# An encoder layer's MLP epilogue: squares and gate inputs of one chunk in instructions of 512 columns, one to a step

## The chip, the cores and the metric

The kernel runs on one core of a Trainium2 chip. The metric is device time in microseconds (us) of one launch; the time before is the median of three runs. A profile is one execution recorded instruction by instruction, with its own time. The engines are TensorE (PE, with its weight loads shown as PEld), VectorE (DVE), ScalarE (ACT), GpSimd (POOL) and SyncE (SP), which here issues the DMAs. Each engine works through its own instructions in program order.

## The reference

One layer of an encoder, applied to two sequences (512 and 1024 tokens, 1536 in all) with shared weights; the model width is 1024.

```python
h = h + concat(attention, pooling) @ w_out
m = _rmsnorm(h, norm_mlp_g)
h = h + jnp.square(jax.nn.relu(m @ w_up)) @ w_down
gate = jax.nn.sigmoid(_rmsnorm(h, norm_ple_g) @ w_ple_gate)
h = h + gate * (p_i @ w_ple_proj)
y = _rmsnorm(h, final_norm_g)
```

What matters here is the seam between the third and the fourth line. When the MLP of some tokens is done, the new `h` has to be squared and summed over the width (for the RMSNorm in front of the gate), and multiplied by the gain `norm_ple_g` (the gate's input).

## The kernel before

**Tiling.** The 1536 tokens form three chunks `c` = 0, 1, 2 of 512 tokens. `h` lies transposed: `hT[c][a]`, with `a` from 0 to 3, is a tile of 128 x 1024 numbers, two blocks `e` = 0, 1 of 128 channels by 512 tokens. A float32 product is made of three matmuls on float32r parts, a high and a low part of each operand (`three`); so every operand has to be split, high part on ACT by a rounding copy, low part on DVE or POOL by a subtraction. All working tiles come from one pool of 49 slots.

**The MLP loop.** The loop over `pairs` (48 of them, 16 to a chunk, numbered here from 0) does the MLP: a pair is two blocks of 128 columns of `w_up`. `Pair.run` forms the up-projection with seven half-size block products in the order 1, 6, 2, 5, 7, 3, 4 (PSUM tiles `px`, `py`, `px`, `pz`, `pq`, `pz`, `pq`), combines them on DVE into `c1` and `c2`, applies relu and square on ACT, and subtracts on DVE to get the low part of the result `r` (L886). Four times in a pair `between` is called, which runs `before.down(i)`: a quarter of the down-projection of the previous pair, into `pd`, added to `h` on DVE (L837). The first of these quarters, after product 1, is the first reader of the `r` that the pair before has just made: ahead of it lie c1's and c2's relu and squares (L875 to L877, L881 to L883) and L886.

**Steps.** After each of the seven products `after(i)` is called. It takes one piece of the stream that splits the next pair's up weights (`feeding`, ACT cast L786, POOL subtraction L787), one of the splits of the down weights, and one `step()`. `step()` advances the first generator in the queue `chores` by one `yield`. So a pair has seven steps; this text calls them places 0 to 6, place 0 being `after(1)`, place 4 `after(7)`, place 5 `after(3)` and place 6 `after(4)`. When a generator is used up, the same step already begins the next one in the queue.

**What is in the queue.** At the second pair of a chunk `c` (pairs 1, 17, 33) the queue gets, in this order: `invert(c)`, four steps; `finishing(c - 1)` if there was a chunk before; and `make_m(c + 1)` if there is a chunk after. `finishing` closes the MLP of the chunk before: for each of the four tiles it scales `h` back by `ws` (L1138, two instructions of 512 columns, one to a step), writes it out to DRAM (`hl_d`), squares it on ACT (L1142), and from the second tile on adds the square to a running sum on POOL (L1147, two steps). For chunk 0 it also makes the gate's input, high part on ACT (L1126) and low part on DVE (L1128, two steps), and writes both to `hg_d`. At the end come the last sum (L1155), waits of some steps, and `spread_g`, which turns the sum into a row of reciprocal roots. `make_m(c + 1)` prepares the MLP input of the next chunk in two halves of 22 steps: loads, squares (L607, L609), gains, differences, and the splits into `mm` (ACT L637, POOL L634), written to `mo_d`; then, seven steps on, a product for the sum, L646 on DVE, and the write of `w_d` (L647).

**The end of a chunk.** In the last pair of a chunk `after(i)` also loads the operands of the next chunk's products (`load_mo`, from `mo_d`). At the start of the next chunk `h` is loaded, `load_ms` loads `w_d` into `ws`, and `raise_h` multiplies `h` by it on DVE (L662). All these DMAs are issued by SP in program order.

Of the kernel before, what the change touches and what calls it, by code (L numbers as in the profile page):

```python
# [11 lines left out]
AF = mybir.ActivationFunctionType  # L12
# [23 lines left out]
def encoder_layer(ctx, tc, xT, xn, xr, pT, w1, w2, w_pool, w_out, w_up, w_down, w_gate, w_proj,  # L36
# [7 lines left out]
    ve, sc, gp, sy = nc.vector, nc.scalar, nc.gpsimd, nc.sync  # L44
# [15 lines left out]
    def as32(ap):  # L60
        return ap.bitcast(F32)

    def flat(ap):
        return as32(ap).rearrange("p a b -> p (a b)" if len(ap.shape) == 3 else "p a b c -> p (a b c)")
# [9 lines left out]
    def slot(shape, dt, name):  # L74
        n = math.prod(shape[1:])
        full = slots.tile([P, SLOT], dt, tag="s", name=name)
        v = full[:, 0:n]
        if len(shape) == 3:
            v = v.rearrange("p (a b) -> p a b", a=shape[1])
        elif len(shape) == 4:  # L80
            v = v.rearrange("p (a b c) -> p a b c", a=shape[1], b=shape[2])
        return v
# [432 lines left out]
    def wait(n):  # L515
        for _ in range(n):
            yield
# [165 lines left out]
    def spread_g(c, acc):  # L683
        bc = yield from rsqrt_rows([acc[:, 0]], CH, f"g{c}")
        if c != 1:
            bcs["t"] = slot([P, 2, CH], F32, f"bcs{c}")
        sc.copy(bcs["t"][:, c % 2], bc)
        bcs[c] = bcs["t"][:, c % 2]
        yield
# [428 lines left out]
    def gate_in(c, a, high=None, hs=range(2)):  # L1118

        if (c, a) not in gin:  # L1120
            gin[c, a] = [slot([P, 2, CH], F32R, f"hg{c}{a}_{i}") for i in range(2)]
        hl = gin[c, a]
        for h in hs:
            g = gple_sb[:, 2 * a + h:2 * a + h + 1]
            if high is not False:
                sc.activation(hl[0][:, h], hT[c][a][:, h], AF.Copy, scale=g)  # L1126
            if not high:
                ve.scalar_tensor_tensor(hl[1][:, h], hT[c][a][:, h], g, as32(hl[0][:, h]), op0=ALU.mult, op1=ALU.subtract)  # L1128

    hl_d = [[dram.tile([P, 2, CH], F32, name=f"hl_d{c}_{a}") for a in range(4)] for c in range(2)]  # L1130
    def finishing(c):


        acc = slot([P, 2, CH], F32, f"sqg{c}")
        for a in range(4):
            h = hT[c][a]
            for e in range(2):
                ve.tensor_tensor(h[:, e], h[:, e], ws[c], op=ALU.mult)  # L1138
                yield
            sy.dma_start(hl_d[c][a], h)  # L1140
            sq = slot([P, 2, CH], F32, f"sqg{c}{a}") if a else acc
            sc.activation(sq, h, AF.Square)  # L1142
            if c == 0:
                gate_in(0, a, True)
            yield
            for e in range(2) if a else ():
                gp.tensor_tensor(acc[:, e], acc[:, e], sq[:, e], op=ALU.add)  # L1147
                yield
            if c == 0:
                for e in range(2):  # L1150
                    gate_in(0, a, False, (e,))
                    yield
                for i in range(2):
                    sy.dma_start(hg_d[a][i], flat(gin[c, a][i]))
        gp.tensor_tensor(acc[:, 0], acc[:, 0], acc[:, 1], op=ALU.add)  # L1155
        yield from wait(6)
        yield from spread_g(c, acc)
# [22 lines left out]
    for n, pair in enumerate(pairs):  # L1180
        c, g = pair.c, pair.g
# [7 lines left out]
        if g == 1:  # L1189
            chores.append(invert(c))  # L1190
            if c:
                load_ms(c - 1)
                chores.append(finishing(c - 1))
            if c < 2:
                chores.append(make_m(c + 1, ve, gp))
# [105 lines left out]
    for c, o, w in groups:  # L1301
        sq = []
# [94 lines left out]
```

## Time and profile before

| What | Value |
|---|---|
| Time, median of 3 runs | 1814.47 us (1813.41 to 1815.92) |
| The profiled execution's own time | 1813.31 us |
| Its span | 1811.5 us |
| PE busy | 1759.7 us, 97% of the span |
| DVE, POOL, ACT busy | 1260.0, 1053.7 and 939.7 us |
| The eight squares of L1142, mean of one | 1058 ns |
| The 24 high parts of L1126, mean of one | 711 ns |

Times within the span are counted from its start. The MLP loop runs from about 579 us to 1620 us; chunk 1 begins at about 923 us and chunk 2 at about 1270 us. A row of a timeline gives start, duration, engine, line, operation, output and inputs, the number of instructions merged, and in brackets the idle time of the engine just before with what ended it. A row of windows gives for a stretch the busy time of each engine. Busy times can include waits of a pipelined matmul, so the distance between the same product of two pairs says more about PE's pace than its busy share.

### The profile page before, as it was taken

To read this page: it belongs to the slowest core of one execution; us is meant where nothing else is said; L and a number is where in the kernel's file an instruction comes from. 1 tells how busy PE (TensorE), PEld (TensorE's weight loads), DVE (VectorE), ACT (ScalarE), POOL (GpSimd) and SP (SyncE) were. 2 spreads that over 40 slices of the span, in tenths; PEclk is the share of its full clock that TensorE was granted. 3 is DMA by queue.
4 is the path that set the end of the run, shared out by engine and by line. 5 is a ranking of instruction groups with operands and counts; after the bars stand their busy time and mean duration, and the time that the engine had idled before them with its cause. 6 is when DMAs were issued, how large, how long until landed. Compare 5 with 4: busy or idle time off the path is not lost.

```text
span 1811.5 us, 28604 instructions
## 1 busy us (share of the span) xinstructions
PE 1759.7 (97%) x10540; PEld 1537.1 (85%) x10540; DVE 1260.0 (70%) x1843; ACT 939.7 (52%) x1854; POOL 1053.7 (58%) x923
## 2 busy tenths in 40 slices
PE   9999899999999799999999999999999999999997
PEld 7888777888868798988888889889898999888887
DVE  5677865888894677865568877876776556665655
ACT  6434455768794455655445545554455444443332
POOL 3474774535674567676656776785577666543121
PEclk9999999999999899999999999999999999999998
DMA  6333545120519335343364442556443323272102
GB/s 248 114 123 105 216 165 185 36 94 13 206 46 367 139 122 198 121 177 100 136 265 157 163 151 96 195 185 235 179 157 100 110 94 99 89 262 70 59 12 82
DMA packets 83883, 256.84 MB, mean 142 GB/s; under 512 B 9888, under 2 KB 16416, under 8 KB 83744
## 3 DMA queue, kind: packets, MB, share of 16 engines
q1 hardware_dynamic: 83744, 255.02, 39.7%
q8 instruction: 83, 1.36, 0.3%
q14 instruction: 56, 0.46, 0.1%
HBM read 195.74 MB, written 59.24 MB: 141 GB/s over the span
## 4 chain that ended last, share of the span: by engine, by line
PE 78%; DVE 7%; ACT 5%; DMA 3%; issue 3%; POOL 1%; POOLq 0%; DVEq 0%; ACTq 0%; SPq 0%
PE pd L49 25%; PE z L49 7%; PE px L49 6%; PE pz L49 6%; PE pq L49 6%; PE pg L49 6%; PE py L49 4%; PE pp L49 3%; PE o L49 3%; PE tp L53 3%; PE po L49 3%; PE S L49 3%; PE pj L49 1%; DMA wur<-in_w_up_dram 1%; DVE r L886 1%
## 5 line engine op out<-in xcount | busy, mean ns | idle before, releaser
L49 PE MATMUL pd<-r,wd 128*128 128x512 f32 x2304 | 568.5, 395 | 10.8 <-DVE r L886 10.6
L49 PEld LDWEIGHTS pd<-r,wd 128*128 128x128 f32 x2304 | 419.5, 188 | 100.3 <-DVE r L886 16.1
L787 POOL TENSOR_TENSOR w<-ws,w 128x512 fp32r<-128x512 f32 x192 | 272.5, 1423 | 217.9 <-ACT w L786 206.8
L787 POOL TENSOR_TENSOR w<-wur,w 128x512 fp32r<-128x512 f32 x144 | 212.8, 1489 | 135.4 <-ACT w L786 134.4
L837 DVE TENSOR_TENSOR h<-pd,h 128x1024 f32<-128x1024 f32 x192 | 233.5, 1216 | 76.6 <-PE pd L49 76.5
L786 ACT CAST w<-ws 128x512 fp32r<-128x512 f32 x192 | 118.5, 617 | 271.1 <-DVE ws L795 241.1
L461 POOL TENSOR_SCALAR pr<-pr,rr 128x512 f32<-128x512 f32 x160 | 111.2, 705 | 134.7 <-DVE rr L456 66.8
L49 PE MATMUL z<-w,x 128*128 128x512 f32 (+1 forms) x864 | 175.7, 359 | 0.9 <-DVE w L160 0.5
L49 PEld LDWEIGHTS pz<-mo,w 128*128 128x128 f32 x1152 | 150.7, 190 | 19.3 <-issue 11.2
L49 PEld LDWEIGHTS z<-w,x 128*128 128x128 f32 x864 | 142.9, 189 | 28.0 <-ACT w L159 2.1
L49 PE MATMUL pz<-mo,w 128*128 128x256 f32 x1152 | 153.6, 283 | 10.2 <-issue 10.2
L817 DVE TENSOR_TENSOR wd<-wdr,wd 128x512 fp32r<-128x512 f32 x96 | 102.8, 1071 | 83.1 <-ACT wd L816 76.6
L49 PE MATMUL pq<-mo,w 128*128 128x256 f32 x1152 | 153.7, 283 | 1.0 <-issue 1.0
L49 PE MATMUL px<-mo,w 128*128 128x256 f32 x1152 | 152.2, 281 | 0.0
L49 PEld LDWEIGHTS px<-mo,w 128*128 128x128 f32 x1152 | 146.5, 189 | 4.0
L49 PEld LDWEIGHTS pq<-mo,w 128*128 128x128 f32 x1152 | 144.7, 191 | 1.4 <-issue 1.3
L49 PE MATMUL pg<-hg,wg 128*128 128x512 f32 (+1 forms) x768 | 141.0, 338 | 0.2
L472 ACT CAST pt<-tp 128x512 fp32r<-128x512 f32 x160 | 88.0, 591 | 88.5 <-PE tp L53 86.8
L49 PEld LDWEIGHTS pg<-hg,wg 128*128 128x128 f32 x768 | 118.6, 188 | 17.8 <-DVE hg L1128 1.0
L817 POOL TENSOR_TENSOR wd<-wdr,wd 128x512 fp32r<-128x512 f32 x96 | 131.8, 1373 | 2.6 <-DMA w_d<-sqm 2.6
L886 DVE TENSOR_TENSOR r<-c,r 128x512 fp32r<-128x512 f32 x96 | 74.7, 783 | 74.1 <-ACT c L883 46.2
L473 DVE TENSOR_TENSOR pt<-tp,pt 128x512 fp32r<-128x512 f32 x160 | 104.0, 684 | 31.4 <-ACT pt L472 31.1
(195 smaller groups left out, 3036.2 us busy)
## 6 DMA issues: line engine op xcount, KB each, us to landing
wur<-in_w_up_dram SPq DMA_DIRECT2D x96, 512.0 KB, 4.2
wdr<-in_w_down_dram SPq DMA_DIRECT2D x96, 512.0 KB, 4.4
mo_d<-mm SPq DMA_DIRECT2D x84, 256.0 KB, 2.3
mo<-mo_d SPq DMA_DIRECT2D x42, 512.0 KB, 7.7
h_d<-h SPq DMA_DIRECT2D x16, 512.0 KB, 3.0
h<-h_d SPq DMA_DIRECT2D x16, 512.0 KB, 9.9
xn<-in_xn_dram SPq DMA_DIRECT2D x12, 512.0 KB, 6.4
qs_d<-qs SPq DMA_DIRECT2D x12, 512.0 KB, 3.0
```

What stands on the lines that cost most here:

```text
L49: last_pe[0] = nc.tensor.matmul(*a, **k).ins
L53: last_pe[0] = nc.tensor.transpose(*a, **k).ins
L461: gp.tensor_scalar(p, p, rr, 1.0, op0=ALU.mult, op1=ALU.mult)
L472: sc.copy(self.pt[kt][:, 0], tp)
L473: ve.tensor_tensor(self.pt[kt][:, 1], tp, as32(self.pt[kt][:, 0]), op=ALU.subtract)
L786: sc.copy(t[:, 0], x)
L787: gp.tensor_tensor(t[:, 1], x, as32(t[:, 0]), op=ALU.subtract)
L817: (gp, ve)[i].tensor_tensor(lo, self.dr[i][:, h], as32(hi), op=ALU.subtract)
L837: ve.tensor_tensor(h, pd.rearrange("p (a b) -> p a b", a=2), h, op=ALU.add)
L886: ve.tensor_tensor(self.r[i][:, 1], x, as32(self.r[i][:, 0]), op=ALU.subtract)
```

## The change

In `finishing` the square of a tile, one instruction of 1024 columns, becomes two of 512 columns, each with a step of its own. For chunk 0 the two instructions that make the high part of the gate's input, issued before in the same step as the square, get a step each as well.

```diff
             sy.dma_start(hl_d[c][a], h)
             sq = slot([P, 2, CH], F32, f"sqg{c}{a}") if a else acc
-            sc.activation(sq, h, AF.Square)
-            if c == 0:
-                gate_in(0, a, True)
-            yield
+            for e in range(2):
+                sc.activation(sq[:, e], h[:, e], AF.Square)
+                yield
+            for e in range(2) if c == 0 else ():
+                gate_in(0, a, True, (e,))
+                yield
             for e in range(2) if a else ():
                 gp.tensor_tensor(acc[:, e], acc[:, e], sq[:, e], op=ALU.add)
                 yield
```

`gate_in(0, a, True, (e,))` issues L1126 for the block `e` alone. Nothing else is changed, and the numbers computed are the same. `finishing(0)` has 38 steps in its four tiles where it had 26, `finishing(1)` 22 where it had 18; chunk 2 doesn't use `finishing`.

## The prediction

> **What bounds the kernel now.** I read the page first, then the stretch in which `finishing` runs, by waits, by the timeline and by the distance of equal products. The page:
>
> ```profile
> span 1811.5 us, 28604 instructions
> PE 1759.7 (97%) x10540; PEld 1537.1 (85%) x10540; DVE 1260.0 (70%) x1843; ACT 939.7 (52%) x1854; POOL 1053.7 (58%) x923
> ```
>
> PE sets the time: only what makes it wait can be won back, and a change on ACT alone is worth nothing where PE runs on. The waits between 950 and 1070 us, where `finishing(0)` runs, show what is to be won there (total, times, longest):
>
> ```profile
> PEld pd L49 <- DVE r L886: 4.8, 3, 1.8
> ```
>
> Three times the down-projection waits for the low part of `r`. One of the three, in pair 20, from the timeline of all engines:
>
> ```profile
> 1028.22 0.62 ACT L786 CAST w<-ws 128x512 fp32r<-128x512 f32 x1 [4.49 <-DVE ws L795]
> 1028.75 1.06 ACT L1142 ACTIVATE sqg<-h 128x1024 f32<-128x1024 f32 x1
> 1029.25 0.41 DVE L874 TENSOR_TENSOR c<-pz,u 128x256 f32<-128x256 f32 x1
> 1029.71 1.32 ACT L1126 ACTIVATE hg<-h,gple_sb 128x512 fp32r<-128x512 f32 x2
> 1030.93 0.40 ACT L875 ACTIVATE c<-c 128x256 f32<-128x256 f32 x1
> ...
> 1033.71 1.27 PE L49 MATMUL pd<-r,wd 128*128 128x512 f32 x4
> 1034.46 0.63 ACT L883 ACTIVATE c<-c 128x512 f32<-128x512 f32 x1
> 1034.63 1.27 POOL L1147 TENSOR_TENSOR sqg<-sqg,sqg 128x512 f32<-128x512 f32 x1
> 1035.12 1.32 DVE L886 TENSOR_TENSOR r<-c,r 128x512 fp32r<-128x512 f32 x1 [1.61 <-ACT c L883]
> 1036.50 2.15 PE L49 MATMUL pd<-r,wd 128*128 128x512 f32 x8 [1.52 <-DVE r L886]
> ```
>
> The relu L875 has its input at 1029.66 (1029.25 + 0.41), but ACT has the step's square and two gate inputs in front of it and starts L875 at 1030.93: 1.27 us late. From there ACT has no pause up to L883, DVE subtracts last, and PE stands for 1.52 us. In pairs 18, 19 and 20 this step falls on place 4, just ahead of that chain; in pair 17 on place 6, behind it, and PE doesn't wait.
>
> What a pair loses is read from the distance of its first `px` to that of the next pair. The rows below are those of pairs 2 and 5, 19 to 22, 26 and 27, 36 and 37:
>
> ```profile
> 624.85 1.60 PE L49 MATMUL px<-mo,w 128*128 128x256 f32 x12
> ...
> 688.15 1.58 PE L49 MATMUL px<-mo,w 128*128 128x256 f32 x12
> ...
> 987.06 1.59 PE L49 MATMUL px<-mo,w 128*128 128x256 f32 x12
> 1009.22 1.57 PE L49 MATMUL px<-mo,w 128*128 128x256 f32 x12
> 1032.29 1.59 PE L49 MATMUL px<-mo,w 128*128 128x256 f32 x12
> 1055.34 1.57 PE L49 MATMUL px<-mo,w 128*128 128x256 f32 x12
> ...
> 1141.05 1.56 PE L49 MATMUL px<-mo,w 128*128 128x256 f32 x12
> 1163.96 1.59 PE L49 MATMUL px<-mo,w 128*128 128x256 f32 x12
> ...
> 1356.92 1.57 PE L49 MATMUL px<-mo,w 128*128 128x256 f32 x12
> 1379.17 1.57 PE L49 MATMUL px<-mo,w 128*128 128x256 f32 x12
> ```
>
> Pairs 2, 3 and 4 take (688.15 - 624.85) / 3 = 21.10 us each: an undisturbed pair. The three pairs from 987.06 to 1055.34 take 68.28, which is 4.98 more than 3 x 21.10. The pair at 1356.92, in `finishing(1)`, takes 22.25, so 1.15 too many. The pair at 1141.05, in `make_m(2)`, takes 22.91 and loses 1.81.
>
> **The change part by part.** First the work itself, from the groups with each shape apart:
>
> ```profile
> L1126 ACT ACTIVATE hg<-h,gple_sb 128x512 fp32r<-128x512 f32 x24 | 15.3, 711 | 0.0
> L607 ACT ACTIVATE sqm<-m 128x512 f32<-128x512 f32 x24 | 15.2, 634 | 0.0
> L1142 ACT ACTIVATE sqg<-h 128x1024 f32<-128x1024 f32 x8 | 8.5, 1058 | 0.0
> ```
>
> Removed are 8 squares of 1058 ns; added are 16 of 634 ns (L607 is the same operation at 512 columns): 10.1 for 8.5 us, 1.7 us more ACT work over some 20 pairs, where ACT is little over half busy. Its price is nothing as long as no piece stands in the chain ahead of L886.
>
> [...]
>
> *finishing(0): 4.98 us, of which 4.4 go.* The 2.4 us lump becomes four steps of 0.63 or 0.71. Counting yields from place 0 of pair 17 (four of `invert`, then 8 for the first tile and 10 for each other, two of them L1138 ahead of the square), the four ACT steps fall on these places: first tile 6, 0, 1, 2; second 0, 1, 2, 3; third 3, 4, 5, 6; fourth 6, 0, 1, 2. Places 6 and 0 to 3 are covered: the chain is over by then, and ahead of place 4 ACT idles 4.49 us (the first row of the timeline). The third tile, in pair 20, keeps 0.63 on place 4, which fits the 0.8 us between the end of L786 (1028.84) and L875's input (1029.66), and 0.71 on place 5, which does not fit anywhere. Without the lump (1.27) and without the POOL sum beside L886 (0.63, see below) `r` would come 1.90 earlier, 0.38 ahead of need; so 0.71 leaves 0.33 of waiting. In pair 19 the sum L1147 still falls on place 5: of a wait like that of 1.52 us the lump's 1.27 go and some 0.2 stay. I leave 0.6 in all; bounds 0 and 2.5 (half of what is there).
>
> L886 took 1.32 us in the timeline above, beside L1147 on POOL. Where POOL is free it takes 0.69:
>
> ```profile
> 1229.15 0.69 DVE L886 TENSOR_TENSOR r<-c,r 128x512 fp32r<-128x512 f32 x1 [1.62 <-ACT c L883]
> ```
>
> So a moved POOL sum has a price of 0.63 us where it meets L886.
>
> *finishing(1): 1.15 us, of which 1.0 go.* The one square that hurt fell on place 5. Now the squares fall on places 6, 0; 3, 4; 2, 3; 1, 2, all covered as above; 0.15 stays for a sum on place 5.
>
> *make_m(2) starts 12 steps later: 1.81 go, 0.8 come.* It is next in the queue, 38 steps instead of 26 ahead of it, so it begins on place 3 instead of 5. Its second half then lies on the places that the first half of `make_m(1)` has, which lost nothing in pairs 2, 3 and 4 (the first two `px` rows above).
>
> For the first half no row shows the new places. It has a gain step (two ACT instructions, 1.42 us) on place 5, against a reserve of about 1.1 us, since four `pd` matmuls run before the low part is needed (1.27 us in the timeline of pair 20). That and a split on place 5 cost some 0.3 to 1.0; bounds 0 and 1.8, as now. I take 0.8, so 1.0 is won.
>
> *The end of chunk 1: 2.1 us come.* `make_m(2)` writes `w_d` in its step 52. Counted from pair 17 that was step 91, place 0 of pair 30, and is now step 103, place 5 of pair 31, two steps before the next chunk loads it. The order on SP before, and what hung on it:
>
> ```profile
> 1232.20 0.33 SPq L647 DMA_DIRECT2D w_d<-sqm x1
> ...
> 1261.92 0.81 SPq L56 DMA_DIRECT2D wur<-in_w_up_dram  x2
> 1264.52 1.59 PE L49 MATMUL pz<-mo,w 128*128 128x256 f32 x12
> ...
> 1266.87 2.82 SPq L56 DMA_DIRECT2D h<-h_d  x4
> 1270.69 0.32 SPq L56 DMA_DIRECT2D w<-w_d  x1
> 1280.34 1.14 DVE L662 TENSOR_TENSOR h<-h,w 128x512 f32<-128x512 f32 x1 [7.16 <-DMA w<-w_d]
> 1286.31 1.64 PE L49 MATMUL pz<-mo,w 128*128 128x256 f32 x12 [0.52 <-issue]
> ```
>
> DVE stands 7.16 us at L662 until `w` has landed, runs all its delayed work, and PE already waits for it; so a later `w` costs PE as much. The write now goes into SP's queue ahead of the `wur` pair at 1261.92 and waits for L646 behind the product that ends at 1266.1 and two matmuls more: about 1267.5. SP is blocked until then, and `wur`, `mo`, `h` and `w` go out later. The chain of waits has `w` issued when `wur` had landed, and the page gives a `wur` load that meets no crowd:
>
> ```profile
> 1261.92 8.71 DMA wur<-in_w_up_dram
> wur<-in_w_up_dram SPq DMA_DIRECT2D x96, 512.0 KB, 4.2
> ```
>
> Issued at 1267.9 behind the 0.6 us of `w_d`'s bytes, `wur` lands at 1267.9 + 0.6 + 4.2 = 1272.7 instead of 1270.63: `w` comes 2.1 us later. Bounds: 0.6 (the bytes alone, the queue never empty) and 6 (all of SP's delay).
>
> *The other moved steps.* The DVE parts L1138 and L1128 and the writes of `hg_d` go to other places and up to 12 steps later. `hg_d` is first read in the last pair of the loop, and L1128 on place 6 has the 1.61 us that DVE idles before L886. Price nothing; if that cover is gone, at most one L1128 in two pairs.
>
> The sum: 4.4 + 1.0 + 1.0 - 2.1 = 4.3 us less. The profiled execution took 1813.31 us, 1.2 below the median; so 1809.0 for its like, and **1810.2 us** against the median of 1814.47.
>
> **The rivals.** *The end of the chunk costs only its bytes.* The transfers issued before keep the queues full while SP stands; then 0.6 instead of 2.1: 1808.7. For it: the queues were full (last columns: DMA share and GB/s). Against: SP stands some 6 us, and what it issued last before is soon through.
>
> ```profile
> 1264.00:1268.00 4.00, 4.00 (x30) 3.78 (x30) 2.07 (x4) 1.33 (x3) 1.15 (x1) 1.00 1.03 410
> ```
>
> *The waits only move.* The stalls come from the sum of ACT, DVE and POOL work in these pairs, not from the lump; half of 4.98 stays, `make_m(2)` wins nothing, the end costs 2.1: 2.5 + 0.5 - 2.1, so 1813.6, no change. For it: L886's 1.32 us, and the 1.81 us of a pair with no lump. This is also the case in which the change doesn't do what it says.
>
> *More ACT work on the path.* If pieces of the cut squares stand in the chain ahead of L886 after all, their 1.7 us come back as waits of PE: 4.3 - 1.7 = 2.6, so 1811.9. For it: the third tile's pieces on places 4 and 5. Against: 14 of the 16 squares fall elsewhere. [...]
>
> *Slower: the next chunk starts as chunk 0 does.* There the write of `w_d` is issued late and the load has to wait for it:
>
> ```profile
> 575.93 0.32 SPq L647 DMA_DIRECT2D w_d<-sqm x1
> ...
> 585.38 0.33 SPq L56 DMA_DIRECT2D w<-w_d  x1
> 595.48 2.90 PE L49 MATMUL pz<-mo,w 128*128 128x256 f32 x12 [9.20 <-issue]
> ```
>
> Write and load are 9.45 us apart, and PE stands 9.20 us. If chunk 2 pays those 9.2 on top, against 5.4 won in `finishing` and nothing in `make_m`, the time is 1818.3. It decides from the point where `w` lands more than some 9 us later than 1280.3, which needs `w_d`'s own landing to be held up by the chunk's loads. Against it: in front of this write `wur` had landed 8.71 us after its issue, with the same queues, so `w_d` should land by 1276, and `w` not much past 1283.
>
> **How the numbers follow.** Forecast 1810.2 (0.45), bytes only 1808.7 (0.15), moved waits 1813.6 (0.20), ACT work on the path 1811.9 (0.07), slow start 1818.3 (0.13). The forecast's own range is 1808.4 to 1814.8: the bounds of its four terms, added as squares to each side (0.6, 0.15, 0.8, 1.5 below, 1.9, 1.0, 1.0, 3.9 above). About 0.2%, 3.6 us, is what a measurement of this kernel can tell from no change, so below 1810.8 counts as faster. Two thirds of the forecast lie there, nine tenths of the bytes alone and a tenth of the moved waits: 0.30 + 0.14 + 0.02 = 0.46. Slower is the slow start and a little of the moved waits, 0.14; the rest, 0.40, is no change. The range for 8 in 10 goes from the sum of all lower bounds, 1807.2, rounded down to 1807.0, to 1816.5, between the moved waits and the slow start.
>
> **What would show it.** L1142 in 16 instructions of about 0.63 us; in pairs 18 to 20 L875 right behind L874, and the distances of `px` at 21.1 to 21.5; L646 near 1260 (all is some 5 us earlier by then) and the write of `w_d` right behind it, ahead of `wur`; DVE's wait at L662 longer than 7.16 by about two. I'd be wrong if the waits for L886 between 950 and 1070 us stay above 2.5 us, if the first half of `make_m(2)` loses over 1.8, or if `w` lands more than 6 us later against its chunk.

## The result: 1.0% slower, 19 us instead of 4 us the other way

| Kernel | Median, us | Runs | Ratio to before [95%] |
|---|---|---|---|
| before, beside it | 1814.57 | 4 | |
| after | 1833.60 (1832.02 to 1834.67) | 4 | 1.0104 [1.0092, 1.0116] |

The prediction was 1810.2 us, its range 1807.0 to 1816.5. The profiled execution of the changed kernel took 1834.21 us. Its page, to be set against the first two rows of the prediction:

```profile
span 1832.3 us, 28595 instructions
PE 1768.8 (97%) x10540; PEld 1543.3 (84%) x10540; DVE 1251.5 (68%) x1843; ACT 940.5 (51%) x1862; POOL 1047.5 (57%) x923
```

ACT has the 8 instructions more that the change makes (1862 for 1854) and is 0.8 us busier; DVE and POOL have as many as before. So no engine has 20 us more to do, and the 20.8 us by which the span grew are waits, or work at a lower clock (granted over the span: 0.989 on average, before 0.995). The squares themselves, in the groups with each shape apart (total and mean of one in the sixth and seventh place), are as costed:

```profile
L1143 ACT ACTIVATE sqg<-h 128x512 f32<-128x512 f32 x16 | 10.1, 630 | 0.0
```

**Where the time came from.** The rows below are first `px` products of pairs 19 to 21, 24 and 25, 28 and 29, 32 and 33 of the changed kernel. As in the prediction, a pair stands for the stretch from its `px` to the next pair's, and its loss is what that stretch has over 21.10 us.

```profile
987.79 1.59 PE L49 MATMUL px<-mo,w 128*128 128x256 f32 x12
1008.89 1.57 PE L49 MATMUL px<-mo,w 128*128 128x256 f32 x12
1031.80 1.59 PE L49 MATMUL px<-mo,w 128*128 128x256 f32 x12
...
1096.87 1.58 PE L49 MATMUL px<-mo,w 128*128 128x256 f32 x12
1126.69 1.57 PE L49 MATMUL px<-mo,w 128*128 128x256 f32 x12
...
1190.61 1.57 PE L49 MATMUL px<-mo,w 128*128 128x256 f32 x12
1216.49 1.56 PE L49 MATMUL px<-mo,w 128*128 128x256 f32 x12
...
1283.72 1.60 PE L49 MATMUL px<-mo,w 128*128 128x256 f32 x12
1313.75 1.60 PE L49 MATMUL px<-mo,w 128*128 128x256 f32 x12
```

Pair 19 takes 21.10 now and pair 20 22.91 (22.16 and 23.07 before). But pair 24 takes 29.82, pair 28 25.88 and pair 32 30.03: 8.72, 4.78 and 8.93 lost, where the same three lost 0.00, -0.03 and 1.48 before. All pairs read in this way, in groups:

| Pairs | Loss before | Loss after | Difference |
|---|---|---|---|
| 18 to 22, tiles of `finishing(0)` | 6.32 | 2.73 | -3.59 |
| 23 and 24 | 0.06 | 9.60 | +9.54 |
| 25 to 31, `make_m(2)` | 2.44 | 9.33 | +6.89 |
| 32 and 33, start of chunk 2 | 2.46 | 9.28 | +6.82 |
| 36 to 38, `finishing(1)` | 2.38 | 2.26 | -0.12 |
| all others together | | | +0.09 |

The sum is +19.63 us. The stretch that the change edits gained 3.6, of which 0.8 is only a product that went from pair 22 to pair 24 (`bcg`, below); three other places each took about twice that.

**Pair 24: the roots of `finishing(0)`.** PE's waits of the changed kernel (total, times, longest), first in the window of the prediction, then in the 130 us behind it:

```profile
PEld pd L49 <- DVE r L886: 3.1, 3, 1.2
...
PE pd L49 <- DVE r L886: 8.6, 2, 5.4
```

Between 950 and 1070 us the weight loads' waits for L886, the row that the prediction shows, fell from 4.8 to 3.1 us (those of PE itself from 3.7 to 1.9). Behind that window PE has two new ones, 5.4 us in pair 24 and 3.2 in pair 28. The timeline of all engines from the end of pair 23 on:

```profile
1096.58 0.60 ACT L786 CAST w<-ws 128x512 fp32r<-128x512 f32 x1
...
1097.26 1.29 POOL L787 TENSOR_TENSOR w<-ws,w 128x512 fp32r<-128x512 f32 x1 [1.14 <-ACT w L786]
...
1098.51 1.02 POOL L538 TENSOR_TENSOR rsg<-rsg,mhalf 128x4 f32<-128x4 f32 x1
...
1099.62 0.20 POOL L548 TENSOR_SCALAR rhg<-rsg 128x4 fp32r<-128x4 f32 x1
1099.85 2.51 DVE L552 TENSOR_TENSOR dgg<-id_sb,rhg 128x512 fp32r<-128x512 f32 x2 [5.36 <-POOL rhg L548]
...
1102.29 2.35 DVE L886 TENSOR_TENSOR r<-c,r 128x512 fp32r<-128x512 f32 x2
1104.09 5.06 PE L49 MATMUL pd<-r,wd 128*128 128x512 f32 x11 [5.41 <-DVE r L886]
```

`spread_g`, the end of `finishing(0)`, makes reciprocal roots on POOL (L538, L548) and has DVE multiply by them (L552). The added steps put it 12 steps later, on place 6 of pair 23. There L552 comes into DVE's queue ahead of L886. It needs L548; that stands on POOL behind the subtraction L787; that needs ACT's cast L786; and that stands on ACT behind the relu chain. So the low part of `r` waits for the roots: DVE stands 5.36 us, PE 5.41 us. PE's first use of them is later, in the product `bcg`; the view of that tile has start and median of its two matmuls:

```profile
L49 PE MATMUL bcg<-dgg,ones_sb x2: 393/393/393, 1112.2 to 1112.4; 128*128 128x512 f32 x2
```

These 0.79 us are work of PE that lay in pair 22 before and lies in pair 24 now. Before, L552 waited 3.09 us, in pair 22, on place 1 behind L886, and PE ran on. The timeline before:

```profile
1065.20 2.54 DVE L552 TENSOR_TENSOR dgg<-id_sb,rhg 128x512 fp32r<-128x512 f32 x2 [3.09 <-POOL rhg L548]
```

**Pair 28: two waits of DVE for a slot.** DVE's waits in the changed kernel between 1164 and 1200 us, and what follows in the timeline:

```profile
DVE wd L817 <- DMA mo_d<-mm: 4.4, 1, 4.4
DVE ws L801 <- DMA mo_d<-mm: 3.9, 1, 3.9
```

```profile
1193.25 0.69 DVE L801 TENSOR_TENSOR ws<-wur,wur 128x512 f32<-128x512 f32 x1 [3.90 <-DMA mo_d<-mm]
...
1195.66 4.15 PE L49 MATMUL pd<-r,wd 128*128 128x512 f32 x11 [3.24 <-DVE r L886]
```

L801 writes into a slot whose last tile, an `mm` of `make_m(2)`, is still being written out to `mo_d`. Behind L801 stands L886, and PE waits 3.24 us. The size of this loss varies: in the five kernels of this text that leave this part of `make_m(2)` where the change put it, pair 28 loses between 2.81 and 5.75 us.

**Pair 32: `w` lands 7.3 us later.** SP's queue ahead of chunk 2 (the first eight rows), DVE's first L662 and PE's next wait in the changed kernel:

```profile
1254.57 9.59 SPq L636 DMA_DIRECT2D mo_d<-mm  x6
1264.26 0.86 SPq L56 DMA_DIRECT2D wur<-in_w_up_dram  x2
1265.17 3.55 SPq L56 DMA_DIRECT2D mo<-mo_d  x6
...
1280.79 0.32 SPq L647 DMA_DIRECT2D w_d<-sqm  x1
1282.07 1.63 SPq L56 DMA_DIRECT2D wur<-in_w_up_dram  x2
...
1287.20 3.51 SPq L56 DMA_DIRECT2D h<-h_d  x4
1291.62 0.32 SPq L56 DMA_DIRECT2D w<-w_d  x1
...
1301.18 0.69 DVE L662 TENSOR_TENSOR h<-h,w 128x512 f32<-128x512 f32 x1 [14.91 <-DMA w<-w_d]
...
1303.06 5.22 PE L49 MATMUL pd<-r,wd 128*128 128x512 f32 x12 [6.45 <-DVE h L837]
```

L662 starts 17.46 us behind the `px` of its pair (1301.18 - 1283.72); before it was 10.17 (1280.34 - 1270.17). From the issue of `w` to L662 it is 9.56 us (1301.18 - 1291.62), where it was 9.65 (1280.34 - 1270.69): `w` doesn't take longer to land, it is issued later, 7.90 us behind its `px` instead of 0.52. All of DVE's work stands behind it, and PE waits 6.45 us for a freed `pd`. The same queue before, for its start only:

```profile
1246.92 4.88 SPq L56 DMA_DIRECT2D mo<-mo_d  x6
```

The loads of `mo` began 23.25 us ahead of pair 32 before, and 18.55 us ahead of it now, because SP, which works in order, was first busy with the writes of `make_m(2)` to `mo_d`. SP's waits between 1236 and 1284 us have

```profile
SPq L636 <- POOL mm L634: 18.0, 7, 4.1
SPq L647 <- DMA wdr<-in_w_down_dram: 0.9, 1, 0.9
```

The second row is all that SP stands at the write of `w_d`. In the kernel before, the writes to `mo_d` were long done by then: SP's rows that the prediction quotes show `w_d`, which follows them, out at 1232.20.

**What a wait costs on top.** The `pd` products behind these waits are slow. Twelve undisturbed ones of the changed kernel, from its timeline:

```profile
1187.84 2.94 PE L49 MATMUL pd<-r,wd 128*128 128x512 f32 x12
```

That is 0.245 us each, so 2.70 for 11. In pair 24 eleven took 5.06 (2.36 too much), in pair 32 twelve took 5.22 (2.28), in pair 28 eleven took 4.15 (1.45). With the waits and `bcg` this accounts for the three pairs: 5.41 + 2.36 + 0.79 = 8.56 of 8.72, 6.45 + 2.28 = 8.73 of 8.93, 3.24 + 1.45 = 4.69 of 4.78. The windows behind the waits of 5.41, 6.45 and 3.24 us (third column from the right: granted clock):

```profile
1104.00:1108.00 4.00, 3.91 (x9) 3.17 (x10) 2.37 (x4) 1.14 (x2) 0.91 (x1) 0.50 0.13 33
1303.00:1307.00 4.00, 3.94 (x9) 3.14 (x10) 4.00 (x8) 0.00 (x0) 0.00 (x0) 0.50 0.00 1
1195.00:1199.00 4.00, 3.34 (x9) 2.68 (x10) 2.94 (x4) 2.16 (x4) 3.10 (x3) 0.57 0.86 344
```

and that behind the wait of 1.52 us in the kernel before:

```profile
1036.00:1040.00 4.00, 3.50 (x21) 3.12 (x22) 4.00 (x5) 2.05 (x4) 4.00 (x3) 1.00 0.10 40
```

The short wait left the clock at 1.00; behind the three longer ones it was 0.50, 0.50 and 0.57 over 4 us. But length alone doesn't decide. In the kernel with the cut alone (the first experiment below) PE waits the same 1.52 us in the same pair, 21, and the clock falls:

```profile
1037.97 3.44 PE L49 MATMUL pd<-r,wd 128*128 128x512 f32 x8 [1.52 <-DVE r L886]
```

```profile
1038.39:1041.80 3.41, 3.41 (x11) 2.74 (x10) 3.31 (x4) 1.14 (x2) 3.41 (x3) 0.50 0.01 2
```

The eight products took 3.44 us there and 2.15 in the kernel before. How long a stretch at 0.50 is shows in windows that hold one whole, here those of pairs 24 and 32 of the changed kernel:

```profile
1103.00:1110.00 7.00, 5.91 (x17) 4.90 (x18) 4.18 (x5) 1.14 (x2) 2.99 (x3) 0.51 0.31 91
1301.00:1308.00 7.00, 4.94 (x12) 3.90 (x13) 6.82 (x11) 0.00 (x0) 0.00 (x0) 0.51 0.08 32
```

A mean of 0.51 over 7 us is about 6.8 us at 0.50, and that of 0.57 over the 4 us of pair 28, above, about 3.4. In the profiles of the thirteen kernels of this text, between 610 and 1625 us, each of the 13 waits of PE of 2.7 us or more came with a stretch at 0.50, 3.4 or 6.8 us long; of the nine between 1.5 and 1.9 us four did (1.52, 1.75, 1.79 and 1.81 us); of the 19 between 1.0 and 1.5 us none.

### The profile page after: what moved, and what is told of

It is laid out like the page before. It is cut to its first block, busy times and chain, and to the rows that moved or that the text cites. A ratio compares the mean times of both kernels' runs of the same rounds, so it can differ in the third digit from the quotient of the medians.

```text
span 1832.3 us, 28595 instructions
## 1 busy us (share of the span) xinstructions
PE 1768.8 (97%) x10540; PEld 1543.3 (84%) x10540; DVE 1251.5 (68%) x1843; ACT 940.5 (51%) x1862; POOL 1047.5 (57%) x923
## 5 line engine op out<-in xcount | busy, mean ns | idle before, releaser
L49 PE MATMUL pd<-r,wd 128*128 128x512 f32 x2304 | 575.6, 398 | 22.8 <-DVE r L886 15.8
L787 POOL TENSOR_TENSOR w<-ws,w 128x512 fp32r<-128x512 f32 x192 | 270.3, 1411 | 236.1 <-ACT w L786 229.6
L787 POOL TENSOR_TENSOR w<-wur,w 128x512 fp32r<-128x512 f32 x144 | 209.5, 1465 | 143.3 <-ACT w L786 142.5
L786 ACT CAST w<-ws 128x512 fp32r<-128x512 f32 x192 | 118.4, 617 | 276.1 <-DVE ws L795 240.2
L817 DVE TENSOR_TENSOR wd<-wdr,wd 128x512 fp32r<-128x512 f32 x96 | 99.5, 1037 | 94.9 <-ACT wd L816 88.5
L817 POOL TENSOR_TENSOR wd<-wdr,wd 128x512 fp32r<-128x512 f32 x96 | 130.6, 1360 | 2.2 <-ACT wd L816 2.2
L886 DVE TENSOR_TENSOR r<-c,r 128x512 fp32r<-128x512 f32 x96 | 81.4, 856 | 63.3 <-ACT c L883 43.3
```

The source lines that it names most:

```text
L49: last_pe[0] = nc.tensor.matmul(*a, **k).ins
L786: sc.copy(t[:, 0], x)
L787: gp.tensor_tensor(t[:, 1], x, as32(t[:, 0]), op=ALU.subtract)
L817: (gp, ve)[i].tensor_tensor(lo, self.dr[i][:, h], as32(hi), op=ALU.subtract)
L886: ve.tensor_tensor(self.r[i][:, 1], x, as32(self.r[i][:, 0]), op=ALU.subtract)
```

## The experiments

**Is it the cut or the steps?** The change does two things: instructions of half the size, and 12 more steps. Each alone. First the kernel before with the square cut, in the old step:

```diff
-            sc.activation(sq, h, AF.Square)
+            for e in range(2):
+                sc.activation(sq[:, e], h[:, e], AF.Square)
```

> The squares cut in two, but all four ACT instructions still in one step, so nothing in the queue moves. Theory (the extra steps cost the time, by what they push back): within 2 us of the kernel before, 1813 to 1817. Rival (the cut instructions cost it): most of the 19 us is there, above 1825.

Measured: 1816.68 us, 1.0009 [0.9999, 1.0018]. The cut costs between nothing and 0.2%. In its profile pair 21 loses 3.72 (1.95 before) and all others are as they were within 0.4. That is not the 1.7 us of more ACT work, since PE's wait in pair 21 is 1.52 us as before; it is the lower clock behind it, shown above. The 19 us are elsewhere. Then the kernel before with its square whole and the steps alone, empty ones behind the lump:

```diff
             yield
+            yield from wait(1 if c else 3)
```

> The instructions of the kernel before, whole squares and gate inputs in one step, followed by three empty steps in finishing(0) and one in finishing(1): 38 and 22 steps as in the changed kernel. Theory (what comes later in the queue is pushed back by 12 steps): 1832 to 1838, with pairs 24, 28 and 32 long by about 8.7, 4.8 and 8.9 us as in the changed kernel. Rival (the cut instructions): 1813 to 1817.

Measured: 1833.58 us, 1.0100 [1.0085, 1.0115], that is the time of the changed kernel; pairs 24, 28 and 32 lose 8.62, 5.75 and 7.97. **The whole loss comes from the places on which later work falls;** the cut squares and gate inputs add nothing that shows. Nor do they bring the gain: with the squares whole, in a lump that the added steps put on places 6, 0, 3 and 6, pairs 18 to 22 lose 2.13 in all, against 2.73 with them cut and 6.32 before. Both are a matter of places, so the three places can be tried one by one.

**The roots back.** The changed kernel with `spread_g` four steps earlier and `make_m(2)` left where the change put it:

```diff
-        yield from wait(6)
+        yield from wait(6 if c else 2)
         yield from spread_g(c, acc)
+        yield from wait(0 if c else 4)
```

> The changed kernel, with four of the six waits ahead of the row of roots of finishing(0) moved behind it: the roots fall on place 2 instead of 6, make_m(2) starts in the same step. Theory (DVE stands at L552 in front of L886 only on place 6): pair 24 loses under 2 instead of 8.7 us, the rest stays, 1825 to 1828. Rival (the roots cost the same wherever they lie, or something else fills that pair): 1832 to 1835.

Measured: 1826.42 us, 1.0060 [1.0045, 1.0075]. Pair 24 goes from 8.72 to 0.53, pair 23 from 0.88 to 1.79, pairs 28 and 32 still lose 4.45 and 7.34. 7.2 us of the loss hang on the place of one step (1833.60 - 1826.42).

**The write of `w_d` earlier.** Only the last step of `make_m(2)` comes three steps earlier, which was meant to test the prediction's account of pair 32:

```diff
-        yield from wait(7)
+        yield from wait(4 if c == 2 else 7)
```

> The changed kernel, with four instead of seven waits ahead of the sum of make_m(2): w_d is written in step 100, place 2 of pair 31, instead of 103, place 5. Theory (SP stands at the late write, and all loads behind it are late): pair 32 loses 1.5 to 4 instead of 8.9 us, 1826 to 1829. Rival (the loads of the next chunk are late because the writes of mo_d fill the queues just before): pair 32 stays above 7, 1831 to 1835.

Measured: 1830.77 us, 1.0088 [1.0073, 1.0103]. Pair 32 loses 8.89, as before the edit, with `w_d` written 11.51 us ahead of its pair instead of 2.93. **How late `w_d` is written is not what pair 32 pays for.** The edit doesn't rule out that SP can stand at this write: there it now waits for L646, 3.7 us where it was 0.9, with loads of `mo` behind it.

```profile
SPq L647 <- DVE sqm L646: 3.7, 1, 3.7
```

The median is 2.8 us below that of the changed kernel all the same. In its profile pairs 16, 24 and 28 lose 0.25, 7.62 and 2.83 instead of 1.45, 8.72 and 4.78. The edit moves nothing there; behind the wait in pair 28, 1.64 us here, the clock did not fall, and its mean over the span is 0.990, that of the changed kernel 0.989.

**The rest of the shift taken back.** The changed kernel with four and with five of the twelve steps taken out of the wait ahead of `spread_g`, so that `make_m(2)` moves with it. With five, it runs on the places that it had before, one pair later:

```diff
-        yield from wait(6)
+        yield from wait(6 if c else 2)
```

> As the run that moved the roots to place 2, without the four waits behind: make_m(2) starts in step 48 instead of 52, place 6; its last write of mo_d is in step 92, w_d in step 99. Theory now (SP is held by the writes of mo_d that wait for POOL, so the loads of the next chunk start late and share the queues with wur): pair 32 loses 2 to 5 instead of 7 to 9 us, 1820 to 1824. Rival (the late w_d alone, however little earlier): above 7 as with w_d in step 100, 1826 or more.

```diff
-        yield from wait(6)
+        yield from wait(6 if c else 1)
```

> The changed kernel with one wait instead of six ahead of the roots of finishing(0): everything behind finishing lies on the places of the kernel before, exactly one pair later; w_d in step 98. Theory (places decide within make_m, and the nearness of its end to the chunk's decides the rest): pair 28 has no loss of 4.8, some pair loses about 1.8 as pair 26 before; pair 32 2 to 4; 1814 to 1819. Rival (pushing back costs by itself, whatever the places): 1822 or more.

| Loss of pair | after | four steps less | five steps less |
|---|---|---|---|
| 23 | 0.88 | 1.80 | 3.00 |
| 24 | 8.72 | 0.50 | 0.00 |
| 28 | 4.78 | -0.01 | -0.02 |
| 30 | 1.47 | 4.07 | 0.44 |
| 31 | 2.46 | 0.39 | 0.48 |
| 32 | 8.93 | 6.55 | 4.50 |
| Time, us | 1833.60 | 1818.80 | 1818.24 |
| Ratio [95%] | 1.0104 | 1.0025 [1.0014, 1.0037] | 1.0023 [1.0014, 1.0032] |

Pair 28's loss is gone on both, so it hangs on the place of `make_m(2)`. With four steps less a wait of the same kind comes up two pairs on (L801 stands 2.5 us for a slot, and PE then 1.8 us in pair 30); on the old places it doesn't, and pair 27 loses 1.70 there as pair 26 did before. The 3.00 of pair 23 with five steps less has a cause of its own: PE waits 1.39 us for the last sum on POOL, which only one step now separates from the roots.

Pair 32 goes down as `make_m(2)` starts earlier, but even seven steps late it is 3.0 above its old 1.48. I had expected 2 to 5 us in pair 32 with four steps less and 2 to 4 with five; both, 6.55 and 4.50, lie above. In these two kernels the last write to `mo_d` is issued some 34 us ahead of the pair, against 20 in the changed kernel. But SP now stands at the write of `w_d` until L646 is done, with loads of `mo` behind it, and `w` is issued 4.0 us behind its `px` in both. SP's wait, with four and with five steps less:

```profile
SPq L647 <- DVE sqm L646: 5.6, 1, 5.6
SPq L647 <- DVE sqm L646: 4.2, 1, 4.2
```

No run takes this wait away by itself. That pair 28's wait is for slots whose tiles leave late is seen in the trace alone; no run changed the slots or the writes by themselves.

**`make_m(2)` first.** If it is lateness that hurts pair 32, the order of the queue should matter more than any place:

```diff
             chores.append(invert(c))
+            if c < 2:
+                chores.append(make_m(c + 1, ve, gp))
             if c:
...
                 chores.append(finishing(c - 1))
-            if c < 2:
-                chores.append(make_m(c + 1, ve, gp))
```

> The changed kernel with make_m(c + 1) ahead of finishing(c - 1) in the queue: make_m(2) begins in step 4 as make_m(1) does, and the 12 more steps push back nothing but finishing's own end, the roots on place 1. Theory (the loss is what stands behind finishing in the queue): pairs 24, 28 and 32 lose under 2 each, 1808 to 1813. Rival (the cut finishing disturbs what runs beside it, or holding h of chunk 0 longer leaves too few slots): 1818 or more.

Measured: 1825.05 us, 1.0063 [1.0050, 1.0077], far above what the theory gave. Pair 32 loses 0.26, less than in any kernel so far: **its loss comes from `make_m(2)` being late.** But pairs 20 to 24 lose 5.18, 1.70, 1.45, 4.59 and 2.27. The waits in that stretch, between 1005 and 1095 us:

```profile
DVE wd L817 <- POOL mm L634: 5.4, 1, 5.4
ACT w L786 <- POOL mm L634: 5.3, 2, 3.0
```

L817 and L786 wait for L634 of `make_m(2)`, the subtraction that makes the low parts of `mm` and reads its sources. By their operands neither uses its result, so they wait for a slot that it still holds. That slots are short because `finishing(0)`, now behind, keeps chunk 0's `h` in the pool was the rival named above; it fits, but no run shows it.

**`w` ahead of `h`.** What pair 32 waits for is a small load that stands behind four large ones in SP's queue. The changed kernel with `load_ms(c)` in front of the loads of `h`:

```diff
         if g == 0:
+            load_ms(c)
             if c:
...
-            load_ms(c)
             raising = raise_h(c)
```

> The changed kernel, with the load of w at the start of a chunk ahead of the four loads of h. Theory (PE's wait in pair 32 is the landing of w, which stands in full queues behind 2 MB of h): L662 starts 3 to 6 us earlier against px, pair 32 loses 3 to 6 in place of 8.9, 1828 to 1831. Rival (w_d's own write is what is waited for, and SP then holds the loads of h behind it): pair 32 stays above 8, 1833 or more.

Measured: 1826.50 us, 1.0067 [1.0051, 1.0082], better than expected. Pair 32 loses 3.50 instead of 8.93, pair 16 0.00 instead of 1.45. Rows of its timeline:

```profile
1287.28 0.32 SPq L56 DMA_DIRECT2D w<-w_d  x1
1287.69 1.81 SPq L56 DMA_DIRECT2D h<-h_d  x4
...
1294.39 0.69 DVE L662 TENSOR_TENSOR h<-h,w 128x512 f32<-128x512 f32 x1 [10.09 <-DMA h<-h_d]
```

L662 starts 12.65 us behind its `px` (1281.74) instead of 17.46, and waits for `h` now.

**The gain without the shift.** Back to the prediction's first term. The kernel before with the lump of square and gate inputs moved whole to place 6, and the sum and the low part in one step each, so that `finishing(0)` keeps its 26 steps; `finishing(1)` gets one step more, 19 for 18:

```diff
+            yield from wait(2 if a and c == 0 else 1 if a == 3 else 0)
             sc.activation(sq, h, AF.Square)
...
-            for e in range(2) if a else ():
-                gp.tensor_tensor(acc[:, e], acc[:, e], sq[:, e], op=ALU.add)
-                yield
-            if c == 0:
-                for e in range(2):
+            for e in range(2):
+                if a:
+                    gp.tensor_tensor(acc[:, e], acc[:, e], sq[:, e], op=ALU.add)
+                if c == 0:
                     gate_in(0, a, False, (e,))
+                if a or c == 0:
                     yield
```

> Whole squares as in the kernel before and as many steps (26 and 18), but in finishing(0) two waits ahead of the lump of the second to fourth tile, made good by doing a POOL sum and a low part in one step: the lump falls on place 6, behind the chain, and nothing after it is pushed back; in finishing(1) the last square goes from place 5 to 6 by one wait. Theory (the lump costs by its place alone): pairs 19 to 21 lose under 1 in place of 5.0 us, pair 36 under 0.3, so 1809 to 1811.5. Rival (the ACT, DVE and POOL work of those pairs costs it, wherever it lies): 1813 to 1816.

Measured: 1812.17 us, 0.9986 [0.9977, 0.9994]. Pairs 19 to 21 lose 0.99, 1.97 and 0.36 (1.06, 1.97 and 1.95 before). PE's waits for L886 between 950 and 1070 us, 3.7 before, are gone but for 0.2; another has come:

```profile
PE pq L49 <- DVE c L870: 2.1, 2, 1.4
PE pd L49 <- DVE r L886: 0.2, 1, 0.2
```

The three pairs still lose 3.3 us, where I had expected under 1: of the 4.98 only 1.7 are won. What is left may come from the sums and low parts, now together, which slow DVE ahead of L870. So in the next kernel the sums are held back and put on places 3 and 4 of the next pair, with `wait(5)` for `wait(6)` to keep the roots in place (core of the edit):

```diff
+                if c == 0 and e:
+                    add()
                 yield
...
+            if a and c == 0:
+                add()
+                yield
+                yield
             sc.activation(sq, h, AF.Square)
...
+            if a:
+                sums.extend((lambda e=e, sq=sq: gp.tensor_tensor(acc[:, e], acc[:, e], sq[:, e], op=ALU.add)) for e in range(2))
...
-        yield from wait(6)
+        yield from wait(6 if c else 5)
```

Here `add()` issues the next sum in the list `sums`.

> As the run with the lump on place 6 and the steps of the kernel before, but the two POOL sums of a tile on places 3 and 4 of the next pair, where POOL idles, in place of 0 and 1 beside the low parts. Theory (what was left in pairs 19 and 20 of that run, 3.0 us, is POOL slowing DVE, so that PE waits for L870): pairs 19 to 21 lose under 1 in all, 1808.5 to 1811. Rival (DVE's own scalings and low parts cost it, wherever the sums lie): 1811.5 to 1813.5, as that run.

Measured: 1809.96 us, 0.9977 [0.9968, 0.9986]; pairs 19 to 21 lose 0.07, 0.57 and 0.36, so 4.0 of the 4.98 are won, and nothing is lost behind. PE's wait for L870 falls from 2.1 to 0.2 us, so it was the sums. This is nearly the time that was predicted, but by another kernel, which leaves every later step on its place but for the end of `finishing(1)`, one step late. Last, the same with `w` ahead of `h`:

```diff
         if g == 0:
+            load_ms(c)
             if c:
...
-            load_ms(c)
             raising = raise_h(c)
```

> The lump on place 6 with the sums on places 3 and 4, and w ahead of h as well. Theory: pairs 32 and 33 lose 0 to 1 in place of 2.5, 1806 to 1809.5, and faster than without the exchange by 1.5 to 3. Rival (h then comes late in place of w): no difference to the run without it.

Measured: 1806.90 us, 0.9957 [0.9944, 0.9969], the fastest of all, 3.1 us below the kernel without the exchange and faster than the kernels before and after the change. Pairs 16, 17, 32 and 33 lose 0.00, 0.13, 0.06 and 0.27 (before 1.46, 0.84, 1.48, 0.98). Its timeline has

```profile
1269.96 0.77 DVE L662 TENSOR_TENSOR h<-h,w 128x512 f32<-128x512 f32 x1 [3.43 <-DMA h<-h_d]
```

L662 starts 6.43 us behind its `px` at 1263.53, and DVE waits 3.43 us for it, not 7.16.

## Why the prediction was wrong

*`finishing(0)`: 4.4 of 4.98 to go.* 3.1 went; pairs 19 and 21 lose 0.00 and 0.05, pair 20 still loses 1.81. That the lump costs by its place was right: the kernels with the lump on place 6 confirm it, and so does the one with empty steps alone, where pairs 19 and 21 lose 0.01 and -0.03. But then moving it was enough, and the cut gave nothing. The residue was mis-sized. I had left 0.6, of it 0.33 for pieces on places 4 and 5 of pair 20, which cost nothing that shows (0.05 in pair 21). What stands ahead of pair 20 is a sum and a low part together, in the timeline of the changed kernel:

```profile
1008.39 1.10 DVE L1128 SCALAR_TENSOR_TENSOR hg<-h,gple_sb,hg 128x512 fp32r<-128x512 f32 x1 [1.08 <-PE pd L49]
1008.91 1.74 POOL L1149 TENSOR_TENSOR sqg<-sqg,sqg 128x512 f32<-128x512 f32 x1
1009.42 3.48 DVE L886 TENSOR_TENSOR r<-c,r 128x512 fp32r<-128x512 f32 x2
```

The two L886 take 3.48 us there, where one takes 0.69 with POOL free. L1128 on place 6, which I had put at nothing, stands ahead of them: DVE idles 1.08 us in front of it and not at all behind, so the cover of 1.61 us that I named is used up. How the 1.81 us divide between the sum and L1128 no run shows.

*`finishing(1)`: 1.0 of 1.15 to go.* 0.96 went from pair 36, as worked out. But 0.84 came back in pairs 37 and 38 (1.35 and -0.12 before, 0.93 and 1.14 after), where its `spread_g` now runs four steps later. With `spread_g` one step late instead (the kernel with the sums on places 3 and 4) pairs 37 and 38 lose 1.27 together, for 1.23 before and 2.07 after. I hadn't counted this.

*The other moved steps, "Price nothing": this is the step that failed.* I listed L1138, L1128 and the writes of `hg_d`, and left out the end of `finishing`: L537 to L552, one step whose DVE part waits for POOL. Pairs 23 and 24 lost 9.54 more (0.8 of it `bcg`), more than all that I had on the other side; putting this one step back won 7.2. The prediction had counted places for ACT's pieces, but not for this one: step 48 from place 0 of pair 17 is place 6 of pair 23, which the same counting gives.

*`make_m(2)`: 1.0 won, bounds of its loss 0 and 1.8.* Pairs 25 to 31 lost 6.89 more than before. The first half, which I had priced, did better than I forecast: pairs 25 to 27 lose 0.62, and pair 26 came down from 1.81 to 0.43. The loss is all in the second half and behind it, which I had put at nothing, since it lies on places where the first half of `make_m(1)` lost nothing. Equal places were no reason, for I had weighed ACT's pieces alone, against the reserve ahead of L886. What hurt were a slot freed late (pair 28) and waits in pairs 30 and 31 (1.05 and 2.44 more than before), of which no run isolates the cause.

*The end of chunk 1: 2.1, bounds 0.6 and 6.* It cost 6.82 in pairs 32 and 33, with `w` 7.3 us later. That a later `w` costs PE as much was right; why it is later was wrong. The prediction had SP held by the write of `w_d`; SP stood 0.9 us there, and moving that write alone left pair 32 as it was. SP was held earlier, by the fourteen writes of the second half to `mo_d`, and so `mo`, `wur`, `h` and `w` were all issued later. I had placed only the last step of `make_m(2)` in SP's order, not its other DMAs. The wait that I described does come up, 5.6 and 4.2 us, in the kernels in which `make_m(2)` is less late. With `w` ahead of `h` the loss of pair 32 falls from 8.93 to 3.50.

*The rivals.* The slow start of chunk 2, at 0.13, came nearest, by chance. It named 9.2 us more, and pair 32 lost 8.93, 7.45 more than before. But its condition, a `w` that has to wait for the landing of `w_d`, was not what cost: with 18.75 us between the two issues instead of 10.83 (the kernel with the write earlier) the loss was the same. Its sum, 1818.3, lacked the roots and `make_m(2)`. "The waits only move" had half of 4.98 stay, and 1.86 did. That more ACT work lies on the path is seen nowhere: the changed kernel and the one with empty steps alone take 1833.60 and 1833.58 us. By their runs a cost of 1.7 us can't be ruled out.

*The signs.* Two of the three that I had named for being wrong came: the waits for L886 between 950 and 1070 us stayed at 3.1 us, above 2.5, and `w` landed 7.3 us later against its chunk. The third, a loss of over 1.8 in the first half of `make_m(2)`, didn't. None of them looks at the roots, which cost most.

## What to carry to other kernels

In a queue of steps written by hand, an edit that adds a step moves everything behind it: count the new place of every instruction to the end of the queue, those of DVE that wait for another engine first, and ask what stands behind each of them. If a piece of work has to go elsewhere, move it alone and take the steps back in the next wait (1809.96 against 1833.60 us for nearly the same gain at the squares). A small load that a whole engine waits for goes ahead of the large ones: here that gave 7.1 us in the changed kernel and 3.1 in the fastest.

## What was not expected of the hardware

A wait of PE can have a price beyond its length: behind waits of 5.41, 6.45 and 3.24 us in the changed kernel the next `pd` products took 2.36, 2.28 and 1.45 us more, at a granted clock of 0.50 to 0.57. Short waits can have it too. The wait of 1.52 us in pair 21 was followed by a granted clock of 1.00 in the kernel before and of 0.50 with the cut alone, and the pair lost 1.95 us in the one and 3.72 in the other. What decides between the two is not shown.
